# Residual transfers on GpSimd's queue, a buffer of their own for growing sums, a convolution that runs on into the last gate, and the output's first products by quarters

## The chip, the cores and the metric

The kernel runs on one core of a Trainium2 chip. TensorE (PE) multiplies, VectorE (DVE), ScalarE (ACT) and GpSimd (POOL) do the rest, and SyncE (SP) issues transfers. The metric is the device time of one execution in microseconds; of several runs the median is taken.

## The reference

A trunk of two layers (DEPTH = 2) over 512 tokens of 1024 channels, in float32. Cut to what matters here:

```python
for l in range(depth):
    h = _rmsnorm(x, g_mix[l])
    proj = h @ w_in[l]              # gates of 4 branches | conv | three attentions
    ys = jnp.stack([y_a, y_b, y_c, y_d], axis=2)   # conformer conv, three attentions
    branch = jnp.einsum('bsnc,ncd->bsnd', ys, w_branch[l])
    gates = jax.nn.sigmoid(gate_pre.reshape(bsz, seq, 4, 1024) + gate_b[l])
    mixed = jnp.sum(gates * branch, axis=2)
    x = x + mixed @ w_out[l]
    x = x + _conv_ffn(_rmsnorm(x, g_ffn[l]), w_up[l], ffn_conv_w[l], ffn_conv_b[l], w_down[l])
```

The FFN has 2816 channels in each half: up-projection, a depthwise convolution of width 3, silu(gate) times up, and the down-projection.

## The kernel before, in words

All activations lie transposed: 128 channels on the partitions, 512 tokens along the row, so the 1024 channels are eight tiles (d = 0 to 7). A float32 product is made of three products of rounded parts: `hi` (rounded) and `lo` (the rest), hi*hi + hi*lo + lo*hi. Each weight tile is loaded as `w_raw`, rounded on ScalarE into `w_hi` (L245 or L271), and VectorE makes `w_lo` (L247 or L272). `w_raw` is a ring of two tiles, `w_hi` and `w_lo` rings of three.

A layer runs: the norm and its projections; convolution and attentions as generators on a list `side`, of which `tick()` takes one step between matmuls; the gates of three branches; then `last_gate_and_out()`; then the norm of the FFN, its up-projections (44 blocks of 24 matmuls in `ffn`, two per step i) and the down-projection.

The last gate (keys `0a`, `0b`) and the output projection (`oa`, `ob`) are matrix products of 2 by 2 blocks in seven products instead of eight, in the order of the list LAST. A11, A12 and A22 use quarters of the weight as loaded. S3, S2 and S4 use sums of quarters, which grow in a tile `chain`: the first quarter comes from SyncE, each next one is added in place by an accumulating DMA on GpSimd (`grow`, L252). S1 uses the tile that A22 was loaded into, grown by another quarter; in the kernel before it is a `w_raw` tile. The activations' side needs sums as well: `input_forms` loads the residual (`xf`, L916) and makes `form` tiles for the last gate; `mixed_forms(j)`, called for each pair of mixed rows (j = 0 to 3, each 256 of the 1024 contracted channels), makes the `sums`, their rounded parts `mform` and the rounded rows `mpart` (L948, L949). A matmul of these products is at L972, 128 by 256.

`last_out` adds the residual (`xr`, loaded at L1070, added at L1057), stores the new one (`res`, L1063) and calls `norm_tile`, which makes `xh`, `xl` and the square `sq`. `broadcast_norm` then sums the squares over the partitions (L385), and takes three Newton steps for the inverse root on VectorE (`ms`, `rs_q`, `RB`, L389 and L329 to L334). The up-projections multiply unnormed data, and RB is applied when a block leaves PSUM (U, L1181). Four banks may wait for that. `weight_sums` reads four quarters of a down-projection weight (`quad`, L1237), forms their sums on VectorE (L1244 to L1247) and stores them (L1250) for later.

The order of the instructions on each engine is settled when the program is built: a scheduler places them by data and priority. Engines then run their rows in that order and wait for each other by semaphores. A DMA is a row on the queue of the engine that issues it.

## Time and profile before

| what | value |
|---|---|
| median of three runs | 1609.56 us (1606.7 to 1610.41) |
| profiled execution | 1608.74 us, its span 1607.0 us |
| mean granted TensorE clock | 0.986 |
| busy PE, DVE, ACT, POOL | 1564.0, 1322.6, 898.4, 199.5 us |
| `xf`, `xr` loads and `res` stores | 24 in each layer, 256 KB each, on SyncE |

The span is the time between the first and the last instruction that the profiler saw; the device time stands 1.74 us above it. "Busy" counts matmuls in a pipeline, so TensorE at 97% still has places in which it waits, and stretches at a lowered clock.

### The profile page before, as it was taken

Reading aid. Unit: us, or ns where it says so; the run is one execution under the profiler, and the core shown is the slowest. Engines: PE = TensorE matmul, PEld = TensorE weight load, DVE = VectorE, ACT = ScalarE, POOL = GpSimd, SP = SyncE. Lnnn points to the kernel's source line nnn. Section 1 sums busy time; section 2 is a strip of 40 time slices with the busy share of each in tenths; the row PEclk is TensorE's granted clock in tenths of the full one; section 3 lists DMA queues with packets and bytes.
Section 4 is the critical chain, followed back from the end, with each engine's and each line's share of the span. In section 5 each row is a group of like instructions: output and inputs, shape, how many; then the busy total and the mean of one; then the engine's idle time right before and its main releaser. Section 6 shows DMA issues by size and latency. Waiting matters only on the chain.

```text
span 1607.0 us, 21849 instructions
## 1 busy us (share of the span) xinstructions
PE 1564.0 (97%) x7698; PEld 1319.2 (82%) x7698; DVE 1322.6 (82%) x2236; ACT 898.4 (56%) x1516; POOL 199.5 (12%) x332
## 2 busy tenths in 40 slices
PE   9999999999879999999999999999988899999999
PEld 8888888888868888888888888887978788888887
DVE  6699988878779997796676899889696899977964
ACT  5778777455535543454458686764555454443642
POOL 0102002122101111100002020021221011111000
PEclk9999999999899999999999999999998899999999
DMA  7632322657655556576555322226566667655675
GB/s 231 183 106 77 89 74 80 209 131 171 173 182 177 194 187 200 197 235 210 182 184 179 108 79 84 72 87 209 138 165 183 197 199 224 212 197 199 222 222 169
DMA packets 110301, 265.94 MB, mean 165 GB/s; under 512 B 28272, under 2 KB 30192, under 8 KB 110192
## 3 DMA queue, kind: packets, MB, share of 16 engines
q1 hardware_dynamic: 91696, 200.57, 39.4%
q0 software_dynamic: 18208, 63.45, 14.4%
q8 instruction: 61, 1.00, 0.3%
q10 hardware_dynamic: 288, 0.52, 0.1%
q14 instruction: 48, 0.39, 0.1%
HBM read 223.60 MB, written 35.66 MB: 161 GB/s over the span
## 4 chain that ended last, share of the span: by engine, by line
PE 80%; DVE 11%; ACT 4%; DMA 2%; issue 2%; POOL 0%; SPq 0%; ACTq 0%; DVEq 0%
PE mm L302 15%; PE mm L300 15%; PE mm L301 15%; PE aux L972 6%; PE aux L1312 2%; PE aux L1313 2%; PE aux L1314 2%; PE mm L524 2%; PE mm L526 2%; PE mm L525 2%; DVE w_lo L247 2%; PE mm L1313 2%; PE mm L1312 2%; PE mm L1314 2%; PE aux L817 2%
## 5 line engine op out<-in xcount | busy, mean ns | idle before, releaser
L300 PE MATMUL mm<-xh,w_hi 128*128 128x512 f32 x1152 | 451.3, 392 | 15.4 <-ACT w_hi L245 8.2
L302 PE MATMUL mm<-xh,w_lo 128*128 128x512 f32 x1152 | 450.8, 391 | 0.6 <-DVE w_lo L247 0.5
L301 PE MATMUL mm<-xl,w_hi 128*128 128x512 f32 x1152 | 450.5, 391 | 0.0
L245 ACT ACTIVATE w_hi<-w_raw 128x1024 fp32r<-128x1024 f32 (+1 forms) x273 | 284.9, 1044 | 288.5 <-PE mm L301 104.4
L247 DVE TENSOR_TENSOR w_lo<-w_raw,w_hi 128x1024 fp32r<-128x1024 f32 (+1 forms) x273 | 329.7, 1209 | 88.1 <-ACT w_hi L245 84.9
L300 PEld LDWEIGHTS mm<-xh,w_hi 128*128 128x128 f32 x1152 | 217.4, 189 | 61.0 <-ACT w_hi L245 8.6
L302 PEld LDWEIGHTS mm<-xh,w_lo 128*128 128x128 f32 x1152 | 217.2, 189 | 47.3 <-DVE w_lo L247 1.8
L301 PEld LDWEIGHTS mm<-xl,w_hi 128*128 128x128 f32 x1152 | 217.4, 189 | 43.7 <-DVE xl L358 0.2
L895 POOL TENSOR_TENSOR mx<-mx,t 128x512 f32<-128x512 f32 x40 | 64.4, 1636 | 309.1 <-DVE t L894 196.9
L462 DVE SCALAR_TENSOR_TENSOR cv<-cv,prm 128x512 f32<-128x512 f32 x120 | 94.1, 784 | 0.6
L1181 DVE TENSOR_TENSOR U<-mm,RB 128x512 f32<-128x512 f32 x88 | 60.2, 688 | 38.4 <-PE mm L302 38.2
L1184 ACT ACTIVATE cy<-U,prm 128x512 f32<-128x512 f32 x88 | 70.7, 807 | 25.7 <-DVE U L1181 25.7
L524 PE MATMUL mm<-w_hi,xh 128*128 128x512 f32 x192 | 76.4, 398 | 0.4 <-DVE V L652 0.4
L525 PE MATMUL mm<-w_lo,xh 128*128 128x512 f32 x192 | 75.0, 390 | 0.0
L526 PE MATMUL mm<-w_hi,xl 128*128 128x512 f32 x192 | 74.8, 390 | 0.0
L781 ACT ACTIVATE e<-e,rl 128x256 f32<-128x256 f32 (+2 forms) x96 | 57.4, 598 | 21.8 <-DVE rl L780 21.4
L1186 DVE SCALAR_TENSOR_TENSOR cy<-U,prm,cy 128x512 f32<-128x512 f32 x88 | 65.6, 747 | 1.2
L1185 DVE SCALAR_TENSOR_TENSOR cy<-U,prm,cy 128x512 f32<-128x512 f32 x88 | 65.5, 746 | 0.0
L1190 ACT ACTIVATE fth<-cy 128x512 f32<-128x512 f32 x44 | 27.8, 632 | 66.6 <-DVE cy L1186 66.6
L1250 POOL DMA_DIRECT2D sums<-t x44 | 24.0, 546 | 311.4 <-DVE t L1244 292.0
L272 DVE TENSOR_TENSOR w_lo<-w_raw,w_hi 128x1024 fp32r<-128x1024 f32 x32 | 41.8, 1306 | 23.9 <-ACT w_hi L271 23.7
L972 PE MATMUL aux<-mform,w_hi 128*128 128x256 f32 x256 | 53.9, 309 | 5.8 <-DVE mform L949 2.1
(355 smaller groups left out, 3240.5 us busy)
## 6 DMA issues: line engine op xcount, KB each, us to landing
w_raw<-W SPq DMA_DIRECT2D x215, 512.0 KB, 3.7
quad<-W POOLq DMA_DIRECT2D x44, 512.0 KB, 5.2
w_raw<-W SPq DMA_DIRECT2D x66, 256.0 KB, 3.7
chain<-W POOLq DMA_DIRECT2D x24, 512.0 KB, 6.4
sums<-t POOLq DMA_DIRECT2D x44, 256.0 KB, 3.0
sums<-quad POOLq DMA_DIRECT2D x44, 256.0 KB, 3.8
w_raw<-sums SPq DMA_DIRECT2D x44, 256.0 KB, 3.9
w_raw<-sums SPq DMA_DIRECT2D x22, 512.0 KB, 4.6
```

Source lines behind the costliest of these rows:

```text
L245: w = nc.scalar.activation(hi[:, s], raw[:, s], AF.Copy)
L247: nc.vector.tensor_tensor(lo[:, s], raw[:, s], hi[:, s].bitcast(F32), ALU.subtract)
L300: mm(ps, lhsT=wh, rhs=xh, start=start, stop=False)
L301: mm(ps, lhsT=wh, rhs=xl, start=False, stop=False)
L302: self.last_mm = mm(ps, lhsT=wl, rhs=xh, start=False, stop=stop)
L462: self.after_mm(v.scalar_tensor_tensor(acc, u[:, t:t + S], w(t), acc, ALU.mult, ALU.add))
L524: mm(pss[b], lhsT=self.Xh[k][:, t], rhs=hi[:, s], start=k == 0, stop=False)
L525: mm(pss[b], lhsT=self.Xh[k][:, t], rhs=lo[:, s], start=False, stop=False)
L526: self.last_mm = mm(pss[b], lhsT=self.Xl[k][:, t], rhs=hi[:, s], start=False, stop=k == KT - 1)
L972: self.last_mm = self.nc.tensor.matmul(o, lhsT=a[:, s], rhs=x, start=start, stop=j == 3 and i == 2, skip_group_check=True)
L1184: nc.scalar.activation(y, u[:, 1:513], AF.Identity, scale=w(1), bias=self.par('ffn_conv_b', c))
L1186: v.scalar_tensor_tensor(y, u[:, 2:514], w(2), y, ALU.mult, ALU.add)
```

## The change

The residual loads (`xf`, `xr`) and the stores (`res`) are issued by GpSimd instead of SyncE. The tile of A22, which grows into that of S1, is `other`, one tile outside the ring. `form_sums` is a generator that stops after t3, and lays out t3 first; `mixed_forms` first rounds this quarter (256 columns) and the rows, then the other 768 columns, so that ScalarE and VectorE have one more instruction per j. The squares of the FFN norm take four tiles of another pool. The drain of the side generators before the last gate ends when the four forms stand, and what is left of `side` (the convolution) runs on during the gate and is drained after it. S1's sum is taken by halves in `0b` too. The first three output products run over j = 0 and 1, then 2, then 3, instead of 0 and 1, then 2 and 3. The first `weight_sums` comes at i = 1 instead of i = 0. TensorE has 7692 matmuls in both programs.

```diff
--- before.py
+++ after.py
@@ -264,7 +264,10 @@
         if n[0] == 'S':
             raw = self.chains[key] if n != 'S1' else self.others[key]
         else:
-            raw = self.wpool.tile([P, 1024], F32, name="w_raw", tag="w_raw", bufs=2)
+            if n == 'A22':
+                raw = self.op.tile([P, 1024], F32, name="other", tag="other", bufs=1)
+            else:
+                raw = self.wpool.tile([P, 1024], F32, name="w_raw", tag="w_raw", bufs=2)
             nc.sync.dma_start(raw, q[key, int(n[1]) - 1, int(n[2]) - 1])
         hi = self.wpool.tile([P, 1024], F32R, name="w_hi", tag="w_hi", bufs=3)
         lo = self.wpool.tile([P, 1024], F32R, name="w_lo", tag="w_lo", bufs=3)
@@ -362,7 +365,7 @@
             with self.tc.issue_after(self.first_hi.ins):
                 nc.scalar.activation(self.sqacc, xn, AF.Square)
         else:
-            sq = pool.tile([P, S], F32, name="sq", tag=self.sq_tag, bufs=2)
+            sq = pool.tile([P, S], F32, name="sq", tag=self.sq_tag, bufs=4 if self.sq_tag == "cv" else 2)
             nc.scalar.activation(sq, xn, AF.Square)
             nc.vector.tensor_tensor(self.sqacc, self.sqacc, sq, ALU.add)
 
@@ -898,12 +901,13 @@
 
     def form_sums(self, t, b11, b12, b21, b22):
 
-        t1, t2, t3, t4 = (t[:, n * 256:(n + 1) * 256] for n in range(4))
+        t3, t4, t2, t1 = (t[:, n * 256:(n + 1) * 256] for n in range(4))
         p = self.nc.vector.tensor_tensor
         p(t3, b12, b22, ALU.subtract)
-        p(t1, b11, b12, ALU.subtract)
+        yield
         p(t2, t3, b11, ALU.subtract)
         p(t4, b21, t2, ALU.add)
+        p(t1, b11, b12, ALU.subtract)
 
     def input_forms(self):
 
@@ -913,7 +917,7 @@
         for j in range(4):
             x = self.op.tile([P, 1024], F32, name="xf", tag=f"XR{j}", bufs=1)
             for e in range(2):
-                nc.sync.dma_start(x[:, e * S:(e + 1) * S], self.xres[2 * j + e])
+                nc.gpsimd.dma_start(x[:, e * S:(e + 1) * S], self.xres[2 * j + e])
             xs.append(x)
 
         def work():
@@ -923,7 +927,8 @@
                     nc.scalar.activation(x[:, s], x[:, s], AF.Copy, scale=self.par('g_mix', 2 * j + e))
                 yield
                 t = self.op.tile([P, 1024], F32, name="sums", tag=f"mt{j % 2}", bufs=1)
-                self.form_sums(t, *(x[:, n * 256:(n + 1) * 256] for n in range(4)))
+                for _ in self.form_sums(t, *(x[:, n * 256:(n + 1) * 256] for n in range(4))):
+                    pass
                 hi, lo = (self.op.tile([P, 1024], F32R, name="form", tag=f"xf{2 * j + n}", bufs=1) for n in range(2))
                 nc.scalar.activation(hi, t, AF.Copy)
                 nc.vector.tensor_tensor(lo, t, hi.bitcast(F32), ALU.subtract)
@@ -938,20 +943,29 @@
         v = nc.vector
         x, y = self.mixed[2 * j:2 * j + 2]
         t = self.op.tile([P, 1024], F32, name="sums", tag=f"XR{2 + j % 2}", bufs=1)
-        self.form_sums(t, x[:, :256], x[:, 256:], y[:, :256], y[:, 256:])
         tags = [f"mt{2 * j + n}" for n in range(2)] + [f"mb{2 * j + n}" for n in range(2)]
         if j >= 2:
             tags = [f"xf{4 * (j - 2) + n}" for n in range(4)]
         th, tl = (self.op.tile([P, 1024], F32R, name="mform", tag=t, bufs=1) for t in tags[:2])
         bh, bl = (self.op.tile([P, 768], F32R, name="mpart", tag=t, bufs=1) for t in tags[2:])
-        for h, l, s in ((th, tl, t), (bh[:, :256], bl[:, :256], x[:, :256]), (bh[:, 256:], bl[:, 256:], y)):
+
+        def parts(h, l, s):
             nc.scalar.activation(h, s, AF.Copy, scale=0.5)
             v.scalar_tensor_tensor(l, s, 0.5, h.bitcast(F32), ALU.mult, ALU.subtract)
+
+        sums = self.form_sums(t, x[:, :256], x[:, 256:], y[:, :256], y[:, 256:])
+        next(sums)
+        parts(th[:, :256], tl[:, :256], t[:, :256])
+        parts(bh[:, :256], bl[:, :256], x[:, :256])
+        parts(bh[:, 256:], bl[:, 256:], y)
+        for _ in sums:
+            pass
+        parts(th[:, 256:], tl[:, 256:], t[:, 256:])
         self.mforms.append(((th, tl), (bh, bl)))
 
     def seven_x(self, key, n, j):
 
-        form = {'S1': 0, 'S2': 1, 'S3': 2, 'A22': 3}.get(n)
+        form = {'S1': 3, 'S2': 2, 'S3': 0, 'A22': 1}.get(n)
         if form is not None:
             return [t[:, form * 256:(form + 1) * 256] for t in (self.forms[j] if key[0] == '0' else self.mforms[j][0])]
         if key[0] == 'o':
@@ -984,7 +998,7 @@
         w = self.unit()
         for e in range(2):
             self.seven_part(key, n, w, range(4), e)
-            if key == 'ob' and n == 'S1':
+            if key[1] == 'b' and n == 'S1':
                 self.seven_sum(key, n, e)
             if e == 0:
                 self.tick()
@@ -992,7 +1006,7 @@
         if n in ('S3', 'A11'):
             self.seven_copy(key, n)
             return
-        if not (key == 'ob' and n == 'S1'):
+        if not (key[1] == 'b' and n == 'S1'):
             self.seven_sum(key, n)
         done(key, n)
 
@@ -1060,14 +1074,14 @@
         for e in range(2):
             d = 4 * g + 2 * (1 - r) + e
             xn = xr[:, e * S:(e + 1) * S]
-            nc.sync.dma_start(self.xnew[d], xn)
-            self.norm_tile(d, xn, self.op)
+            nc.gpsimd.dma_start(self.xnew[d], xn)
+            self.norm_tile(d, xn, self.gp)
 
     def load_residual(self, q):
 
         x = self.op.tile([P, 1024], F32, name="xr", tag=f"XR{q}", bufs=1)
         for e in range(2):
-            self.nc.sync.dma_start(x[:, e * S:(e + 1) * S], self.xres[2 * q + e])
+            self.nc.gpsimd.dma_start(x[:, e * S:(e + 1) * S], self.xres[2 * q + e])
         self.xrs.append(x)
 
     def last_gate_and_out(self):
@@ -1086,18 +1100,21 @@
             self.seven(key, n, self.last_gate)
         for d in (6, 7):
             self.branch(ORDER[3], d, bu, self.ths[d])
+        while self.side:
+            self.tick()
         for q in range(4):
             self.load_residual(q)
         self.xnew = self.new_res()
+        self.sq_tag = "cv"
         self.start_norm('g_ffn')
         ws = []
+        for js in ((0, 1), (2,), (3,)):
+            for i, (key, n) in enumerate(steps[at:at + 3]):
+                if js[0] == 0:
+                    ws.append(self.unit())
+                for e in range(2):
+                    self.seven_part(key, n, ws[i], js, e)
         for key, n in steps[at:at + 3]:
-            ws.append(self.unit())
-            for e in range(2):
-                self.seven_part(key, n, ws[-1], (0, 1), e)
-        for (key, n), w in zip(steps[at:at + 3], ws):
-            for e in range(2):
-                self.seven_part(key, n, w, (2, 3), e)
             if n != 'A12':
                 self.seven_copy(key, n)
             else:
@@ -1170,7 +1187,7 @@
                 pss.append(self.mm())
                 self.block(pss[s])
                 self.tick()
-            if i % 2 == 0:
+            if i % 2 == 0 and i or i == 1:
 
                 with self.tc.issue_after(self.last_mm.ins):
                     self.weight_sums(l, i // 2)
@@ -1529,7 +1546,7 @@
                 self.after.append(lambda: self.grow(self.chains['0a'], self.quarters[l]['0a', 0, 0]))
                 for _ in third:
                     pass
-                while self.side:
+                while len(self.forms) < 4:
                     self.tick()
                 self.last_gate_and_out()
                 self.broadcast_norm()
```

SyncE's and GpSimd's queues around the stores of layer 0. SyncE before, from the second-last weights of `w_out` to the first weights of the up-projection (L241; L268 loads the blocks of the seven products, L257 starts a chain):

```order
L257 DMA chain<-W 128x1024
L268 DMA w_raw<-W 128x1024 x2
L1070 DMA xr<-xT 128x512 x4
L268 DMA w_raw<-W 128x1024 x2
L1063 DMA res_4400<-xr 128x512
L1063 DMA res_4401<-xr 128x512
L1063 DMA res_4402<-xr 128x512
L1063 DMA res_4403<-xr 128x512
L241 DMA w_raw<-W 128x1024 x3
L1063 DMA res_4404<-xr 128x512
```

Here the first four stores stand ahead of the first three weights of the up-projection. GpSimd before, up to the memsets of U behind which the first two quads come:

```order
L252 DMA chain<-W 128x1024 x2
L252 DMA w_raw<-W 128x1024
L252 DMA chain<-W 128x1024 x2
L252 DMA w_raw<-W 128x1024
L252 DMA chain<-W 128x1024
L1162 MEMSET U_4922 128x1
```

GpSimd has only growing tiles here; `w_raw` is the one that grows from A22 into S1. SyncE after, the same stretch (L271 is the old L268, for `other` and `w_raw`):

```order
L241 DMA w_raw<-W 128x1024
L271 DMA w_raw<-W 128x1024
L271 DMA other<-W 128x1024
L271 DMA w_raw<-W 128x1024
L257 DMA chain<-W 128x1024
L271 DMA w_raw<-W 128x1024 x2
L271 DMA other<-W 128x1024
L241 DMA w_raw<-W 128x1024 x44
```

On SyncE nothing is left but weights. GpSimd after (L1084 is the old L1070, L1077 the old L1063), from the last loads of `xr` to the fourth of the eight stores:

```order
L252 DMA chain<-W 128x1024 x2
L1084 DMA xr<-xT 128x512 x2
L1077 DMA res_4409<-xr 128x512
L1077 DMA res_4410<-xr 128x512
L252 DMA other<-W 128x1024
L252 DMA chain<-W 128x1024
L1077 DMA res_4411<-xr 128x512
L1077 DMA res_4412<-xr 128x512
```

The stores and the xr loads have left SyncE, and stand on GpSimd between the growing tiles and after them. The first quads (L1254, x2) follow the stores and the memsets of U.

VectorE in layer 0, from the sum of squares to the first U. Before (L329 to L334 are the Newton steps, L247 a weight's `w_lo`, L1244 to L1247 the sums of the quad):

```order
L334 SCALAR_TENSOR_TENSOR RB<-rs_q,RB 128x512
L1246 TENSOR_TENSOR t_5026<-quad 128x512
L332 SCALAR_TENSOR_TENSOR rs_q<-RB 128x512
L247 TENSOR_TENSOR w_lo<-w_raw,w_hi 128x1024
L333 TENSOR_TENSOR rs_q<-rs_q,ms 128x512
L1247 TENSOR_TENSOR quad<-quad,t_5026 128x512
L334 SCALAR_TENSOR_TENSOR RB<-rs_q,RB 128x512
L332 SCALAR_TENSOR_TENSOR rs_q<-RB 128x512
L333 TENSOR_TENSOR rs_q<-rs_q,ms 128x512
L334 SCALAR_TENSOR_TENSOR RB<-rs_q,RB 128x512
L247 TENSOR_TENSOR w_lo<-w_raw,w_hi 128x1024
L1181 TENSOR_TENSOR U_4922<-mm,RB 128x512
```

Two weight splits and four sums of the quad (two of them in these rows) stand between the steps. After (L332 to L337 are the Newton steps, L1198 the old L1181, L1261 the old L1244):

```order
L336 TENSOR_TENSOR rs_q<-rs_q,ms 128x512
L337 SCALAR_TENSOR_TENSOR RB<-rs_q,RB 128x512
L335 SCALAR_TENSOR_TENSOR rs_q<-RB 128x512
L336 TENSOR_TENSOR rs_q<-rs_q,ms 128x512
L337 SCALAR_TENSOR_TENSOR RB<-rs_q,RB 128x512
L247 TENSOR_TENSOR w_lo<-w_raw,w_hi 128x1024
L335 SCALAR_TENSOR_TENSOR rs_q<-RB 128x512
L336 TENSOR_TENSOR rs_q<-rs_q,ms 128x512
L337 SCALAR_TENSOR_TENSOR RB<-rs_q,RB 128x512
L1198 TENSOR_TENSOR U_4931<-mm,RB 128x512
L1198 TENSOR_TENSOR U_4934<-mm,RB 128x512
L1261 TENSOR_TENSOR t_5110<-quad 128x512
```

The sums of the quad have gone behind the first two U, and one weight split fewer stands between the steps.

TensorE at the first output products of layer 0. Before, with the numbers of the tiles (`mform_4309` and `_4310`, `mpart_4311` and `_4312` belong to j = 2, `mpart_4380` to j = 3):

```order
L972 MATMUL aux_4416<-mform_4309,w_hi_4319 128x256
L972 MATMUL aux_4435<-mpart_4311,w_hi_4412 128x256
L972 MATMUL aux_4435<-mpart_4312,w_hi_4412 128x256
L972 MATMUL aux_4435<-mpart_4311,w_lo_4413 128x256
L972 MATMUL mm_4455<-mpart_4311,w_hi_4431 128x256
L972 MATMUL mm_4455<-mpart_4312,w_hi_4431 128x256
L972 MATMUL mm_4455<-mpart_4311,w_lo_4432 128x256
L972 MATMUL aux_4416<-mform_4310,w_hi_4319 128x256
L972 MATMUL aux_4416<-mform_4309,w_lo_4320 128x256
L972 MATMUL aux_4435<-mpart_4380,w_hi_4412 128x256
L972 MATMUL mm_4455<-mpart_4380,w_hi_4431 128x256
```

The last two rows belong to j = 3. After (`mpart_4312` and `_4313` belong to j = 2, `mpart_4383` and `_4384` to j = 3):

```order
L986 MATMUL aux_4444<-mpart_4312,w_lo_4422 128x256
L986 MATMUL mm_4464<-mpart_4312,w_hi_4440 128x256
L986 MATMUL mm_4464<-mpart_4313,w_hi_4440 128x256
L986 MATMUL mm_4464<-mpart_4312,w_lo_4441 128x256
L986 MATMUL mm_4464<-mpart_4312,w_hi_4440 128x256
L986 MATMUL mm_4464<-mpart_4313,w_hi_4440 128x256
L986 MATMUL mm_4464<-mpart_4312,w_lo_4441 128x256
L986 MATMUL aux_4444<-mpart_4383,w_hi_4421 128x256
L986 MATMUL aux_4444<-mpart_4384,w_hi_4421 128x256
L986 MATMUL aux_4444<-mpart_4383,w_lo_4422 128x256
L986 MATMUL aux_4444<-mpart_4383,w_hi_4421 128x256
```

Before, the first matmuls of j = 3 stand between those of j = 2, after nine of them; in the new order j = 2 is whole, 18 matmuls, before j = 3 begins.

## The prediction

> **What bounds the kernel now.** I read the head of the page first, then TensorE's waits, then the windows around them, and last the instructions inside four of those windows.
>
> ```profile
> span 1607.0 us, 21849 instructions
> PE 1564.0 (97%) x7698; PEld 1319.2 (82%) x7698; DVE 1322.6 (82%) x2236; ACT 898.4 (56%) x1516; POOL 199.5 (12%) x332
> ```
>
> TensorE is busy 97% of the span. The change adds and removes no matmul, so all that it can win is TensorE's idle time, and the time that matmuls lose to the half clock granted after an idle stretch. Four rows of the waits (us in total, times, longest):
>
> ```profile
> PE mm L300 <- ACT w_hi L245: 8.2, 2, 5.1
> PE aux L500 <- DVE cv L491: 7.5, 2, 3.9
> PE mm L300 <- DVE U L1181: 7.2, 2, 4.1
> PE aux L972 <- DVE sv L1021: 2.6, 2, 1.3
> ```
>
> Each comes twice, once per layer. The fifth place in a layer is where L972 waits several times for the forms of the output's first products. Windows around the five (the third value is PE busy; PEclk is the granted clock, 1.00 being full):
>
> ```profile
> core 0: us, PE busy (x) PEld busy (x) DVE busy (x) ACT busy (x) POOL busy (x), PEclk, DMA share, GB/s
> 324.00:332.00 8.00, 4.06 (x16) 3.10 (x15) 7.34 (x15) 0.98 (x1) 2.46 (x2) 0.79 0.39 129
> 381.00:390.00 9.00, 7.24 (x45) 5.83 (x45) 9.00 (x13) 4.68 (x6) 0.00 (x0) 1.00 0.51 145
> 399.00:417.00 18.00, 13.09 (x64) 11.15 (x63) 13.27 (x20) 8.00 (x11) 2.60 (x3) 0.72 0.55 136
> 442.00:451.00 9.00, 3.78 (x14) 2.82 (x14) 2.78 (x5) 1.06 (x1) 0.00 (x0) 0.81 0.39 153
> 476.00:480.00 4.00, 0.86 (x4) 0.66 (x4) 3.97 (x6) 1.83 (x3) 0.25 (x1) 1.00 0.84 288
> 1121.00:1130.00 9.00, 5.47 (x22) 4.05 (x21) 7.34 (x13) 4.64 (x7) 1.75 (x2) 0.81 0.35 117
> 1179.00:1188.00 9.00, 7.21 (x45) 5.81 (x44) 9.00 (x13) 5.14 (x6) 0.02 (x1) 1.00 0.50 152
> 1198.00:1216.00 18.00, 13.19 (x60) 11.35 (x59) 12.79 (x19) 7.77 (x11) 2.60 (x3) 0.62 0.56 135
> 1241.00:1250.00 9.00, 5.37 (x23) 4.52 (x23) 3.68 (x7) 2.11 (x2) 0.00 (x0) 0.81 0.38 144
> 1273.00:1284.00 11.00, 6.94 (x19) 5.21 (x18) 10.90 (x17) 6.54 (x8) 0.54 (x1) 0.69 0.77 228
> ```
>
> Idle is the width less PE busy: 3.94, 1.76, 4.91, 5.22, 3.14 in layer 0 and 3.53, 1.79, 4.81, 3.63, 4.06 in layer 1, together 36.8 us. The half clock costs at most width times (1 - PEclk): 1.7, 0, 5.0, 1.7, 0 and 1.7, 0, 6.8, 1.7, 3.4, together 22 us. So the ceiling of any gain is 59 us.
>
> **The change part by part.**
>
> *First up-projection weight (windows 442 and 1241).* TensorE waits there for a weight that is still in flight:
>
> ```profile
> 421.70 1.23 DVE L272 TENSOR_TENSOR w_lo<-w_raw,w_hi 128x1024 fp32r<-128x1024 f32 x1 [1.66 <-ACT w_hi L271]
> 427.70 6.62 SPq L1063 DMA_DIRECT2D res<-xr  x4
> 433.45 1.13 DVE w_lo L272
> 433.58 1.16 POOL L1237 DMA_DIRECT2D quad<-W  x2
> 434.62 11.34 DMA w_raw<-W
> 447.17 0.73 PE L300 MATMUL mm<-xh,w_hi 128*128 128x512 f32 x1 [5.12 <-ACT w_hi L245]
> ```
>
> The load leaves at 434.62, when ob's A12 split (433.45 + 1.13) frees its ring slot; A22 holds the other slot until S1 is split. Two 512 KB quads left 1 us earlier, and the load needs 11.34 us. In the new kernel A22 is out of the ring, so the slot of the split at 421.70 is free at 422.93, 11.7 us earlier; the four residual stores no longer stand ahead of it on SyncE; and the quads come behind the eight stores on GpSimd. Even from the old slot, without the quads, the load would make it by 442. The whole loss goes: 5.22 + 1.7 and 3.63 + 1.7 = 12.3 us. I take 11.5, for some clock lost otherwise; at the least 5, if the load still meets other transfers.
>
> *First gate of the FFN norm (windows 476 and 1273).* TensorE has filled its PSUM banks and waits for U, which needs the Newton chain on VectorE:
>
> ```profile
> 472.19 1.22 DVE L247 TENSOR_TENSOR w_lo<-w_raw,w_hi 128x1024 fp32r<-128x1024 f32 x1
> 473.93 0.68 DVE L1247 TENSOR_TENSOR quad<-quad,t 128x512 f32<-128x512 f32 x1
> 477.31 1.22 DVE L247 TENSOR_TENSOR w_lo<-w_raw,w_hi 128x1024 fp32r<-128x1024 f32 x1
> 478.44 1.88 DVE L1181 TENSOR_TENSOR U<-mm,RB 128x512 f32<-128x512 f32 x3
> 479.28 0.47 PE L300 MATMUL mm<-xh,w_hi 128*128 128x512 f32 x1 [3.14 <-DVE U L1181]
> ```
>
> With `weight_sums(0)` one block later, the four quad sums (L1244 to L1247, spaced 0.60) leave this chain, and one of its weight splits (1.13) too: 2.4 + 1.1 = 3.5 us, against a wait of 3.14. Layer 1 loses the same and one transpose less inside (0.6): 4.2 against 4.06, and its 3.4 of half clock with it. I take 3.0 + 6.0 = 9 us, between 5.5 (no clock regained, a split remaining) and 10.6. TensorE's order between the last product of `ob` and the waiting matmul is the same in both kernels, so an earlier start shifts the chain and the wait alike. The delayed first sums are used only in the down-projection, forty blocks later; their delay costs nothing.
>
> *First output products (windows 399 and 1198).* VectorE sets the pace:
>
> ```profile
> 403.87 0.58 PE L972 MATMUL aux<-mpart,w_hi 128*128 128x256 f32 x1 [1.74 <-ACT mpart L948]
> 405.23 0.68 DVE L949 SCALAR_TENSOR_TENSOR mpart<-mx,mpart 128x512 fp32r<-128x512 f32 x1
> 409.22 1.22 DVE L949 SCALAR_TENSOR_TENSOR mform<-sums,mform 128x1024 fp32r<-128x1024 f32 x1
> 412.74 1.28 PE L972 MATMUL aux<-mform,w_hi 128*128 128x256 f32 x4 [1.03 <-ACT w_hi L271]
> ```
>
> The last form is whole only at 410.44. S3 needs a quarter of it; in the new order that quarter and the parts stand ahead of the other 768 columns, and j=3's inputs would be ready at about 406, where the last parts end now (405.23 + 0.68). The products by quarters give 18 more matmuls of 0.12 us (2.2 us) that can run before j=3. Against this stand 8 more instructions each on ScalarE and VectorE (0.1 us or so apiece beyond the columns that they share), and a new tight spot: A22's split can start only when A11's last matmul has freed its slot, twelve matmuls (1.4 us) ahead of use, while a w_hi and a w_lo take 1.06 + 1.22. VectorE's sum of work stays. I take 3 and 4 us, 7 in all, out of 4.9 + 5.0 and 4.8 + 6.8; the ends are 0 (VectorE no earlier) and 16 (three quarters of both).
>
> *Convolution run into the last gate (windows 324 and 1121, and 381 and 1179).* The transposes L500 wait for L491, behind a VectorE chain that began with a late input:
>
> ```profile
> 298.47 8.70 DMA xf<-xT
> 327.63 1.45 DVE L491 TENSOR_SCALAR cv<-aux,mv,rln 128x256 f32<-128x256 f32 x3
> ```
>
> The order of the new kernel puts the same VectorE work ahead of L491 and the first L500 four or five matmuls (some 1 us) earlier on TensorE. So ending the drain early brings no cover. An earlier xf could give 2 us back: its loads now leave from GpSimd instead of behind weights on SyncE. I take 0 for each layer, from a gain of 0.5 to a loss of 1.5. The S1 sum of 0b by halves (L1021, 1.3 us of wait per layer) is still waited for as a pair by S4's first matmul: 0, to a loss of 0.7 per layer.
>
> *Residual transfers on GpSimd.* 48 DMAs leave SyncE for a queue on which the growing sums stand too:
>
> ```profile
> 401.60 9.69 SPq L1070 DMA_DIRECT2D xr<-xT  x4
> 409.60 0.86 POOL L252 DMA_DIRECT2D w_raw<-W  x1 [16.40 <-DVE w_lo L272]
> 417.73 1.06 ACT L271 ACTIVATE w_hi<-w_raw 128x1024 fp32r<-128x1024 f32 x1 [4.07 <-PE aux L972]
> 438.38 1.06 ACT L271 ACTIVATE w_hi<-chain 128x1024 fp32r<-128x1024 f32 x1 [1.56 <-DMA chain<-W]
> L1250 POOL DMA_DIRECT2D sums<-t x44 | 24.0, 546 | 311.4 <-DVE t L1244 292.0 <-DVE t L1246 18.6 <-DVE fl L1294 0.8
> w_raw<-W POOLq DMA_DIRECT2D x8, 512.0 KB, 5.7
> ```
>
> An issue takes 0.546 us, so 48 of them are 26 us on an engine that is 12% busy: off the path by themselves. What matters is the order: two xr loads stand ahead of oa's `other` grow, and today those loads wait for their tiles up to about 411. The grow would leave at 411.5 instead of 409.60 and land 5.7 later, at 417.2; ScalarE takes it at 417.73. Ahead of ob's last grows stand two stores, 1.1 us; the S4 weight arrives at 438.38 today, is split 2.3 us later, and TensorE needs it after 442. Both hide with 0.5 to 1.3 us to spare, so I charge 1.5 us in all for them and the tight spot above, 0 to 6.
>
> The Trainium skill (SBUF — State Buffer, the box "The DVE blocks DMA trap (SWDGE)") speaks against this part: a DMA issued from GpSimd has its descriptors written by GpSimd's cores, and a two-port VectorE instruction can lock them out. The trace does not show it: L1250's issues take 0.546 us on average with VectorE busy 82% of the span. If each moved issue waited out one 1.22 us split, the 48 would cost 85 us of GpSimd instead of 26 by this estimate; the sum above goes by 26.
>
> **Sum.** -11.5 - 9 - 7 + 0 + 1.5 = -26 us. The profiled execution took 1608.74 us, 1.74 around its span of 1607.0; the median of the runs, 1609.56, is 0.8 above it. 1608.74 - 26 + 0.8 is 1583.5 us. With all terms at their good ends it is 1569, at their bad ends 1609.
>
> **The rivals.** *VectorE keeps the pace of the output products*: the quarter form comes no earlier since VectorE comes to them without a gap, the slow clock stays, and the convolution loses 1.5 us per layer. That is -11.5 - 9 + 0 + 3 = -17.5 and 1592 us. For it: DVE is 9.00 of 9.00 busy in the 381 window. Against: of 18 us in the 399 window it is busy only 13.27.
>
> *Nearly the ceiling*: once TensorE no longer stops in 399 to 417, the clock is never lowered there, and 17 of those 21.5 us come back: 1608.74 - 11.5 - 10 - 17 + 0.8 = 1571 us. For it: every window of PEclk below 0.82 lies behind an idle stretch. Against: 476 to 480 lost 3.14 us at clock 1.00, so idle time and lowered clock aren't tied one to one, and the new split stands on the path.
>
> *The transfers share what they shared*: if the load of 11.34 us was slow because of all transfers together and not because of its place, moving 256 KB stores to another queue changes nothing. Then -7 to -10 remain, and 1601 us. For it: at 476 to 480, with quads in flight, the DMA share is 0.84 at 288 GB/s. Against: eight transfers of the same 512 KB from GpSimd land in 5.7 us, half of 11.34, and the free slot lets this one start before the quads. The Trainium skill (DMA: Bandwidth & Descriptors, "Issuing engines are not separate DMA queues") says that DMAs of all issuing engines run on the same 16 DMA engines and interleave, so that another issuer saves only issue time. By it the gain must come from the slot and the order, as I have counted it.
>
> *GpSimd's queue in order blocks the weights* (slower): an xr load or a store waits for VectorE, and the grow behind it with it. There are three such places per layer (oa's `other`, ob's `other`, ob's last chain), hidden by 0.5 to 1.3 us today. Each us beyond is TensorE's. At 6 us late in all six, less the 1 hidden, 30 us are lost: 1583.5 + 30 = 1613 us; below 5.5 us late it doesn't turn the sign. For it: oa's grow clears by only 0.5. Against: the first store leaves at 427.70 today, 11 us before ScalarE takes ob's last chain at 438.38.
>
> **How the numbers follow.** Forecast 1583.5 (its own range 1577 to 1589): 0.52. VectorE's pace, 1592: 0.22. Nearly the ceiling, 1571: 0.12. Transfers unchanged, 1601: 0.08. Blocked queue, 1613: 0.06. A change of 0.2% (3.2 us) is about what a measurement of this kernel can tell. Faster holds the first four but for a part of the last: 0.90; same 0.04; slower 0.06. The range 1571 to 1600 leaves out the slower case, half of the transfers' case and the better half of the ceiling's.
>
> **What the changed profile would show.** Right: no wait of L300 for w_hi L245 near 436, and its load leaving ahead of the first quad; the wait of L300 for U (now L1198) under 1 us; S3, A11 and A12 of oa running through j=2 with PEclk above 0.8 in the window that is 0.72 and 0.62 now; L500's wait unchanged at 3 to 5 us. Wrong: a wait of L986 (the old L972) for w_hi behind a DMA `other<-W` or `chain<-W`, a wait of L500 over 5 us, or the same idle time moved a few matmuls on, which would show as equal windows at other lines.

## The result, and the profile after

The changed kernel takes 1589.15 us (median of four runs, 1586.98 to 1591.63) against 1608.13 us before (1604.49 to 1610.41): ratio 0.9885, 95% interval 0.9859 to 0.991. The forecast was 1583.5 us in a range of 1571 to 1600: the direction and the range held, the gain is 19 us where 26 were forecast. The profiled execution has a span of 1585.2 us, 21.8 less than before; it is the fastest of the four (1586.98 us), so the profiles differ by more than the medians, whose difference is 19.0 us. Both profiles hold 7698 matmuls (not 7692, as the description of the change has it).

The waits of TensorE, with the new line numbers (L503 is the old L500, L986 the old L972, L1198 the old L1181, L303 and L305 the old L300 and L302):

```profile
PE aux L503 <- DVE cv L494: 10.9, 2, 6.0
PE aux L986 <- ACT sv L1017: 4.8, 4, 1.3
PE aux L986 <- DVE sv L1035: 3.2, 2, 1.6
PE mm L305 <- DVE w_lo L247: 2.9, 2, 1.7
PE aux L986 <- DVE mpart L954: 2.9, 2, 1.4
PE aux L986 <- ACT mpart L953: 1.9, 2, 1.0
PE mm L303 <- DVE U L1198: 1.0, 2, 0.7
```

The wait for the first up-projection weight (8.2) has no row any more, that for U has fallen from 7.2 to 1.0, and the wait of the conv transposes has risen from 7.5 to 10.9. The windows around the same five places in each layer:

```profile
322.00:334.00 12.00, 5.99 (x23) 4.62 (x22) 9.79 (x22) 6.54 (x9) 1.80 (x2) 0.72 0.27 87
382.00:390.00 8.00, 5.07 (x34) 3.90 (x32) 8.00 (x13) 4.75 (x7) 0.76 (x1) 1.00 0.50 179
404.00:414.00 10.00, 6.51 (x38) 5.90 (x37) 9.08 (x16) 6.02 (x9) 2.02 (x3) 0.83 0.27 66
440.00:444.00 4.00, 2.33 (x16) 1.80 (x15) 3.78 (x6) 0.12 (x1) 0.00 (x0) 1.00 0.09 7
468.00:470.00 2.00, 1.73 (x9) 1.14 (x7) 1.93 (x4) 0.52 (x1) 0.00 (x0) 1.00 0.77 262
1110.00:1122.00 12.00, 7.12 (x25) 5.29 (x24) 8.52 (x18) 5.79 (x8) 1.27 (x1) 0.72 0.25 87
1172.00:1180.00 8.00, 5.06 (x32) 3.89 (x31) 8.00 (x14) 3.91 (x6) 0.00 (x0) 1.00 0.45 144
1194.00:1202.00 8.00, 4.31 (x20) 3.90 (x20) 6.98 (x13) 4.85 (x8) 2.02 (x3) 0.79 0.19 67
1230.00:1232.00 2.00, 0.77 (x5) 0.66 (x5) 2.00 (x4) 0.00 (x0) 0.00 (x0) 1.00 0.00 0
1258.00:1260.00 2.00, 1.26 (x6) 1.07 (x7) 2.00 (x3) 2.00 (x3) 0.00 (x0) 1.00 0.49 96
```

Read as in the prediction (idle is width less PE busy, the half clock at most width times 1 - PEclk), the two layers together give, in us:

| place | idle, half clock before | idle, half clock after | change | forecast |
|---|---|---|---|---|
| conv transposes | 7.5, 3.4 | 10.9, 6.7 | +6.7 | 0 |
| 0b's second half | 3.6, 0 | 5.9, 0 | +2.3 | 0 |
| output's first products | 9.7, 11.9 | 7.2, 3.4 | -11.0 | -7 |
| first up weight | 8.9, 3.4 | 2.9, 0 | -9.4 | -11.5 |
| first U | 7.2, 3.4 | 1.0, 0 | -9.6 | -9 |
| GpSimd's queue, spread over these | | | | +1.5 |
| sum | | | -21.0 | -26 |

The sum is within 1 us of the span's 21.8, so in sum little is left for the rest of the program. The largest miss against the forecast is the first row.

What holds the transposes up is seen two steps back. GpSimd's queue in layer 0, and VectorE behind it:

```profile
284.63 0.54 POOL L920 DMA_DIRECT2D xf<-xT  x1 [1.38 <-ACT ytmp L830]
297.27 0.91 POOL L252 DMA_DIRECT2D chain<-W  x1 [12.10 <-DMA other<-W]
300.37 0.60 POOL L920 DMA_DIRECT2D xf<-xT  x1
301.52 1.46 POOL L920 DMA_DIRECT2D xf<-xT  x2
310.25 0.72 ACT L927 ACTIVATE xf<-xf,prm 128x512 f32<-128x512 f32 x1 [2.17 <-DMA xf<-xT]
313.44 1.22 DVE L934 TENSOR_TENSOR form<-sums,form 128x1024 fp32r<-128x1024 f32 x1 [3.41 <-ACT form L933]
328.80 0.47 PE L503 MATMUL aux<-cst,cv 128*128 128x128 f32 x1 [6.01 <-DVE cv L494]
```

Five of the eight xf loads leave by 285. Then the first growing sum is at the head of the queue and waits 12.10 us for a weight to land, and the last three loads stand behind it. The first of the three leaves 16 us after the fifth, ScalarE and VectorE wait for them, and VectorE comes late to L494. The same place before:

```profile
298.47 3.42 SPq L916 DMA_DIRECT2D xf<-xT  x5
307.95 0.66 DVE L903 TENSOR_TENSOR sums<-xf 128x256 f32<-128x256 f32 x1 [0.99 <-ACT xf L923]
309.27 0.43 DVE L903 TENSOR_TENSOR sums<-xf 128x256 f32<-128x256 f32 x1 [0.67 <-ACT xf L923]
311.83 1.22 DVE L929 TENSOR_TENSOR form<-sums,form 128x1024 fp32r<-128x1024 f32 x1 [0.33 <-ACT form L928]
328.23 0.69 PE L500 MATMUL aux<-cst,cv 128*128 128x128 f32 x2 [3.94 <-DVE cv L491]
```

The last five xf loads left SyncE in one row from 298.5 on, and VectorE waited 2.0 us in three pieces, where it waits 3.41 now. This is only a part of the longer wait. The first L494 now starts at 328.20 and the first L491 started at 327.63, 0.6 us earlier, while TensorE stands at the transposes at 322.8 (328.80 less 6.01) instead of 324.3. The traces have 1542 matmuls ahead of them in layer 0 where there were 1547, and 5394 where there were 5398 in layer 1. At 0.23 us from one such matmul to the next, the nine that now come behind the waits are 2 of the 3.4 us by which the waits grew.

### The profile page after: what moved, and what is told of

It reads as the page before. It is cut to its first block, busy times and chain, and to the rows that moved or that the text cites. A ratio compares the mean times of both kernels' runs of the same rounds, so it can differ in the third digit from the quotient of the medians.

```text
span 1585.2 us, 21881 instructions
## 1 busy us (share of the span) xinstructions
PE 1551.2 (98%) x7698; PEld 1309.8 (83%) x7698; DVE 1320.5 (83%) x2246; ACT 898.1 (57%) x1524; POOL 223.4 (14%) x380
## 4 chain that ended last, share of the span: by engine, by line
PE 80%; DVE 10%; ACT 4%; DMA 3%; issue 2%; POOL 1%; SPq 0%; ACTq 0%; POOLq 0%; DVEq 0%
PE mm L303 15%; PE mm L305 15%; PE mm L304 15%; PE aux L986 6%; PE aux L1331 3%; PE aux L1330 3%; PE aux L1329 3%; PE mm L527 2%; PE mm L529 2%; PE mm L528 2%; PE mm L1331 2%; PE mm L1329 2%; PE mm L1330 2%; DVE w_lo L247 2%; PE aux L820 2%
## 5 line engine op out<-in xcount | busy, mean ns | idle before, releaser
L305 PE MATMUL mm<-xh,w_lo 128*128 128x512 f32 x1152 | 450.6, 391 | 2.9 <-DVE w_lo L247 2.9
L303 PE MATMUL mm<-xh,w_hi 128*128 128x512 f32 x1152 | 450.2, 391 | 1.0 <-DVE U L1198 1.0
L247 DVE TENSOR_TENSOR w_lo<-w_raw,w_hi 128x1024 fp32r<-128x1024 f32 (+1 forms) x273 | 329.1, 1207 | 79.9 <-ACT w_hi L245 78.8
L305 PEld LDWEIGHTS mm<-xh,w_lo 128*128 128x128 f32 x1152 | 217.0, 188 | 49.5 <-DVE w_lo L247 3.8
L303 PEld LDWEIGHTS mm<-xh,w_hi 128*128 128x128 f32 x1152 | 216.7, 188 | 45.8 <-issue 2.2
L1198 DVE TENSOR_TENSOR U<-mm,RB 128x512 f32<-128x512 f32 x88 | 60.0, 685 | 23.4 <-PE mm L305 23.3
L784 ACT ACTIVATE e<-e,rl 128x256 f32<-128x256 f32 (+2 forms) x96 | 57.4, 598 | 21.8 <-DVE rl L783 21.4
L777 ACT ACTIVATE e<-e,nm 128x256 f32<-128x256 f32 (+2 forms) x96 | 57.6, 600 | 2.7
L805 DVE TENSOR_TENSOR pt<-aux,pt 128x256 fp32r<-128x256 f32 (+2 forms) x96 | 50.8, 530 | 2.4 <-ACT pt L804 1.3
```

The source lines that it names most:

```text
L247: nc.vector.tensor_tensor(lo[:, s], raw[:, s], hi[:, s].bitcast(F32), ALU.subtract)
L303: mm(ps, lhsT=wh, rhs=xh, start=start, stop=False)
L305: self.last_mm = mm(ps, lhsT=wl, rhs=xh, start=False, stop=stop)
```

## The experiments

Two theories for the lost 6.7 us: A, the xf loads are held up in a queue; B, the run-on convolution brings TensorE to L503 sooner. The first two runs undo one part of the change each.

**xf loads back on SyncE.** In `input_forms`:

```diff
-                nc.gpsimd.dma_start(x[:, e * S:(e + 1) * S], self.xres[2 * j + e])
+                nc.sync.dma_start(x[:, e * S:(e + 1) * S], self.xres[2 * j + e])
```

> The changed kernel with the eight xf loads of each layer back on SyncE; xr loads and res stores stay on GpSimd. In the changed kernel the transposes L503 wait 6.0 and 4.9 us for L494 (3.9 and 3.5 before), and with the half clock the two places lose 9.4 and 8.3 us instead of 5.6 and 5.2. Theory A (GpSimd's queue in order): the last xf loads leave late, behind an addition that waits for VectorE, VectorE idles 3.4 us for the forms, and that is the loss. Then the wait comes back to 4 us or less in each layer, and the time falls by 4 to 7 us, to 1582 to 1585 us. Theory B (TensorE reaches L503 earlier, since the convolution runs on into the gate): the wait stays at 5 us or more and the time within 2 us. Half and half: about 5 us of wait, 2 to 3 us of time.

1588.64 us, ratio to before 0.9876 (0.9857 to 0.9895): no different from the changed kernel. The transposes wait 9.9 us in all, 6.9 of it in layer 0 and 3.0 in layer 1. Theory A in this form holds at most in layer 1, where the wait falls from 4.9 to 3.0; in layer 0 SyncE held the loads up just as well. Its queue in layer 0 shows how:

```profile
292.81 0.42 SPq L271 DMA_DIRECT2D other<-W  x1
293.28 0.43 SPq L920 DMA_DIRECT2D xf<-X  x1
297.99 0.33 SPq L241 DMA_DIRECT2D w_raw<-W  x1
298.36 4.14 SPq L920 DMA_DIRECT2D xf<-xT  x7
307.83 0.42 DVE L906 TENSOR_TENSOR sums<-xf 128x256 f32<-128x256 f32 x1 [4.46 <-ACT xf L927]
```

A22 now has its tile as soon as the pool opens, so its 512 KB load is placed ahead of the xf loads; one xf load leaves before the weight that waits, where three did before, and VectorE waits 4.46 us.

**The full drain restored.** Before `last_gate_and_out()`:

```diff
-                while len(self.forms) < 4:
+                while self.side:
```

> The changed kernel with the full drain of the side generators before the last gate, as before the change; all else as changed. Theory B (the run-on convolution costs): the wait of L503 for L494 falls by 1 us or more in each layer, and the time by 2 to 6 us. Theory A (the xf loads on GpSimd cost): the wait stays within 0.5 us of 6.0 and 4.9 and the time within 2 us of 1589. A third case: the run-on was worth something elsewhere in the gate, and the time rises by 2 us or more.

1589.08 us, ratio 0.9885 (0.9868 to 0.9903), the wait 12.2 us in all (5.7 and 6.5; the second is further from 4.9 than theory A had allowed). So the run-on convolution neither costs nor brings anything that these runs can tell, and theory B is refuted. TensorE comes to the transposes of layer 0 as early as in the changed kernel, after 1542 matmuls, so it is not the run-on that brought it there sooner. The next thing to try is the place of the loads in the order.

**xf loads first, on GpSimd.** The changed kernel, with

```diff
-                nc.gpsimd.dma_start(x[:, e * S:(e + 1) * S], self.xres[2 * j + e])
+                with self.first():
+                    nc.gpsimd.dma_start(x[:, e * S:(e + 1) * S], self.xres[2 * j + e])
```

> The changed kernel with the eight xf loads given priority, so that on GpSimd all eight stand ahead of the first two chain grows (in the changed kernel three of them stand behind these, and the first grow waits 12.1 us for loads of A22 and the chain). Theory A, refined (the last xf loads are held up by the grows ahead of them in GpSimd's queue; with xf on SyncE they were held up by the early other load instead, 4.5 us of VectorE idle in layer 0): VectorE's idle time before the forms (3.4 and 2.6 us) goes to under 1 us, the wait of L503 falls by 2 us or more in each layer, and the time by 4 to 8 us, to 1581 to 1585 us. Theory D (the wait of L503 is VectorE's amount of work and TensorE's earlier arrival): VectorE's idle time goes, but the wait falls by less than 1 us in each layer and the time by less than 2 us.

1581.94 us, ratio 0.9834 (0.9813 to 0.9856). GpSimd's queue now reads

```profile
284.76 3.17 POOL L921 DMA_DIRECT2D xf<-xT  x6 [2.44 <-ACT ytmp L830]
297.33 0.91 POOL L252 DMA_DIRECT2D chain<-W  x1 [9.41 <-DMA chain<-W]
```

and the transposes wait half as long, 5.2 us in both layers (the first row of its waits):

```profile
PE aux L503 <- DVE cv L494: 5.2, 2, 3.3
```

VectorE's 3.41 us before the form are gone. The wait fell by 2.7 and 3.0 us, and 7 us of time came back, as refined theory A expected; theory D is refuted. TensorE is at the transposes of layer 0 at 322.9, after 1542 matmuls, as in the changed kernel, so that nearly all of the 2.7 us there is VectorE's: its first L494 starts at 325.6 instead of 328.2.

**xf loads first, on SyncE.** The same with `nc.sync.dma_start` under `with self.first():`.

> The same as the kernel with the xf loads first on GpSimd, but they are first on SyncE's queue, ahead of the chain and other loads. If the place in the order decides and not the queue: the waits of L503 within 1 us in each layer of the 3.3 and 1.8 us with the loads first on GpSimd, and 1580 to 1584 us. If GpSimd's queue is itself better or worse for these loads: a difference of 2 us or more in the wait of a layer. On SyncE the loads stand behind fifteen weights that wait for their ring slots, so they may come some us later; if that matters, VectorE idles again before the forms.

1579.57 us, ratio 0.9824 (0.9809 to 0.9839), the lowest of all kernels run. The wait is 5.0 us in both layers together (3.1 and 1.9), within 0.2 of that with GpSimd. Its queue in layer 0:

```profile
266.76 25.47 SPq L241 DMA_DIRECT2D w_raw<-W  x5
292.32 0.38 SPq L921 DMA_DIRECT2D xf<-X  x1
292.76 3.29 SPq L921 DMA_DIRECT2D xf<-xT  x7
298.31 0.43 SPq L257 DMA_DIRECT2D chain<-W  x1
298.78 0.43 SPq L271 DMA_DIRECT2D other<-W  x1
```

Here too the loads stand behind weights that wait, and leave 11 us later than the first ones on GpSimd; but all eight have left by 296.1, ahead of `chain` and `other`, while the last two of the changed kernel leave from 301.5 on. Which engine issues them makes no difference that these two runs show; when the last of the eight has left does.

**The changed kernel once more**, on the same chip as the run above.

> The changed kernel itself, on the same chip as the two above, for a comparison with them, and to see how steady the half clock is at the output's first products (1.7 us of loss in each layer in its first profile; 0 to 5.1 in the variants with the same instructions there). Expected: 1587 to 1590 us, the same waits within 0.3 us, and half-clock losses that differ from the first profile by some us where the waits don't.

1589.02 us, ratio 0.9885 (0.9868 to 0.9902). The same program, and yet the transposes wait 5.9 and 7.5 us in this profile, where they waited 6.0 and 4.9 in the first. The row of VectorE in layer 1 gives the reason, first in the changed kernel's first profile, then in this one:

```profile
1093.60 1.23 DVE L934 TENSOR_TENSOR form<-sums,form 128x1024 fp32r<-128x1024 f32 x1 [2.61 <-ACT form L933]
```

```profile
1099.29 1.23 DVE L934 TENSOR_TENSOR form<-sums,form 128x1024 fp32r<-128x1024 f32 x1 [6.86 <-ACT form L933]
```

An xf load of this layer took up to 9.2 us to land in the first and 11.0 in the second, and ScalarE waited 4.0 and 7.2 us for such loads. VectorE idled 4 us more, and the transposes waited 2.6 us more. The loss follows the landing of xf. It also means that one profile tells this wait to some 2 us only; the verdicts on the runs with full drain and with xf on SyncE rest on the times beside it.

Four parts were put into the kernel before alone, to size the terms.

**The tile of its own.** A22 in `other`, and the squares in the other pool (`sq` with four tiles, `norm_tile(d, xn, self.gp)`), since the tile has no room otherwise (alone it needs a pool of 100 KB per partition where 96 are left, so that there is no time for it alone):

```diff
+            if n == 'A22':
+                raw = self.op.tile([P, 1024], F32, name="other", tag="other", bufs=1)
+            else:
```

> The kernel before with A22 in a tile of its own outside the ring, and the squares of the FFN norm in the other pool, without which the tile has no room; all transfers stay on SyncE. Slot theory for the first up-projection weight: the ring slot frees the load some 12 us earlier, the first load stands ahead of the stores on SyncE, and the waits of 5.1 and 3.1 us go below 1.5 us each: 7 to 10 us off 1608. Queue theory: half the wait or more remains, 0 to 5 us off. At the conv transposes: SyncE now loads other ahead of the xf tiles; theory A says that the wait of L500 grows by 0.5 to 2 us in a layer, theory B that it stays at 3.9 and 3.5.

1598.8 us, ratio 0.9946 (0.9926 to 0.9967). Its waits:

```profile
PE aux L503 <- DVE cv L494: 10.0, 2, 6.8
PE mm L305 <- DVE w_lo L247: 2.8, 2, 1.7
```

The wait for the weight itself is gone without moving a store; 2.8 us for its `w_lo` are what is left, as in the changed kernel (2.9). The slot theory holds, though one of these waits is 1.7 us, over the 1.5 expected. And the transposes of layer 0 already wait 6.8 instead of 3.9, with all transfers on SyncE: in this layer the tile alone brings the wait of the changed kernel. Layer 1 went from 3.5 to 3.2.

**The transfers on GpSimd**, all 48, and nothing else (three `nc.sync` to `nc.gpsimd`, as in the change).

> The kernel before with the 48 residual transfers on GpSimd's queue, and nothing else. If the transfers share what they shared: within 3 us of 1608 and the wait for the first up-projection weight (5.1 and 3.1 us) within 1 us of before. If SyncE's order was part of that wait: the stores no longer stand ahead, the wait falls by half, 3 to 6 us off. If GpSimd's order in itself blocks: the wait of L500 at the conv transposes rises by 1 us or more in each layer, 2 to 6 us more, and the wait for the first weight hardly moves.

1604.74 us, ratio 0.9978 (0.9964 to 0.9992).

```profile
PE aux L500 <- DVE cv L491: 10.9, 2, 6.3
PE mm L300 <- DVE U L1181: 8.0, 2, 4.3
PE mm L300 <- ACT w_hi L245: 3.4, 2, 1.7
```

Parts of two expectations came true at once: the weight's wait falls by more than half (8.2 to 3.4), and the transposes' rises (7.5 to 10.9), to 4.6 us in layer 0 and 6.3 in layer 1. So the tile delays xf in layer 0, and the move to GpSimd mostly in layer 1. This part alone is worth 0.2%; in the whole change its gain is probably already had by the tile, since both act on the same wait.

**Quad sums one step later.** `if i % 2 == 0 and i or i == 1:` in `ffn`.

> The kernel before with one edit: the first weight_sums comes at i = 1 instead of i = 0. The place is the first U of the FFN (waits of 3.1 and 4.1 us, and 3.4 us of half clock in layer 1). If the four quad sums inside the Newton chain are the cause: waits of 1 us or less each, 6 to 9.5 us off 1608. If the wait comes from the whole chain being late with the first weight: waits of 2.5 us or more remain, less than 4 us off.

1600.76 us, ratio 0.9952 (0.9935 to 0.997). The row of the wait:

```profile
PE mm L300 <- DVE U L1181: 1.8, 2, 1.6
```

Of 7.2 us 1.8 are left, 1.6 of them in layer 1, where 1 or less was expected. The quad sums in the Newton chain were the cause of the rest.

**Products by quarters** alone (`form_sums`, `mixed_forms`, `seven_x` and the loop over `js` of the change).

> The kernel before with the output's first products by quarters: the order of form_sums, the split of mixed_forms, and the products over j = 0 and 1, then 2, then 3. The window around them loses 10.0 us (idle 4.9, half clock 5.1) in layer 0 and 11.7 in layer 1; in the changed kernel 5.2 and 5.4. If this edit alone did it: 5 us off in each layer, 9 to 12 us off 1608. If the run-on convolution, the halves of S1 or the transfers share in it: 3 us off or less in each layer. As to 0b's waits (the window of 1.8 us in each layer, 2.8 and 2.9 in the changed kernel): if the split forms lengthen them, they rise here by 0.5 to 1 us.

1601.69 us, ratio 0.9961 (0.9944 to 0.9978). The window's idle time goes from 4.9 and 4.8 to 3.9 and 4.0 us, and its half clock from 5.0 and 6.8 to 5.1 and 1.7. One of the waits is longer than any before:

```profile
404.87 1.07 PE L983 MATMUL aux<-mpart,w_hi 128*128 128x256 f32 x2 [2.45 <-ACT mpart L950]
```

TensorE waits for the first inputs of j = 3 all the same: VectorE and ScalarE are not there. So here the edit saves 0.8 to 1.0 us of idle time a layer, and 5 us of lowered clock in this profile. But over the whole program this profile lost 22.2 us to the lowered clock, as much as the one of before: what the clock gained here it lost at other places. Where the rest of the 7 us comes from is not shown. 0b's windows stay at 1.6 and 1.5.

**S1's sum whole in 0b**, in the kernel with the xf loads first on GpSimd:

```diff
-            if key[1] == 'b' and n == 'S1':
+            if key == 'ob' and n == 'S1':
```

(and the same condition further down).

> The kernel of the run before it with the xf loads first on GpSimd's queue, and S1's sum of 0b whole again (the change's halves kept for ob alone). The window of the last gate's second half loses 2.8 to 3.0 us per layer in every variant with the change, 1.7 to 1.8 before it and 1.5 to 1.6 with the quarters alone: a new wait of 1.2 us for a copy of ScalarE, and 1.6 instead of 1.3 us for S1's sum. If the halves cause it: 1 us or so less per layer, 1580 us against 1582. If another edit does (the order of mixed_forms together with the convolution): the window keeps 2.7 us or more and the time is within 1.5 us of 1582.

1580.9 us, ratio 0.9834 (0.9818 to 0.985). 0b's windows go from 2.9 and 2.8 to 1.6 us each, so the halves cause that loss: S1's sum is waited for 0.4 us instead of 1.6. The new wait for a copy of ScalarE stays (1.2 us); it is there with the products by quarters alone as well (1.4 and 1.5). But the next window, of the output's first products, idles 4.1 and 4.0 us instead of 3.4 each. 0.6 us a layer remain, and no difference that the times can tell from the 1581.94 with halves.

## Why the prediction was right or wrong

*First up weight, -11.5: right in its cause, 2 too much.* -9.4. The load leaves at 422.36, near the 422.93 that was worked out. What was not charged is the order on ScalarE and VectorE:

```profile
422.36 25.43 SPq L241 DMA_DIRECT2D w_raw<-W  x4
437.50 1.06 ACT L274 ACTIVATE w_hi<-chain 128x1024 fp32r<-128x1024 f32 x1 [1.56 <-DMA chain<-W]
439.06 1.06 ACT L245 ACTIVATE w_hi<-w_raw 128x1024 fp32r<-128x1024 f32 x1
441.66 1.22 DVE L247 TENSOR_TENSOR w_lo<-w_raw,w_hi 128x1024 fp32r<-128x1024 f32 x1
442.94 0.50 PE L305 MATMUL mm<-xh,w_lo 128*128 128x512 f32 x1 [1.67 <-DVE w_lo L247]
```

The load left long before, but the weight's rounding stands behind the last chain's, which waits for its grow, and its `w_lo` comes another 1.5 us after the rounding, behind the chain's and three sums on VectorE. I had looked at that 1.56 us and called it hidden, since nobody needed the chain's product that early; the ones behind it in the queues needed the engines. No run changes this order, so this reading rests on the rows.

*First U, -9: right.* -9.6 in the profile, and with this part alone 6.8 by the medians (1607.6 to 1600.76), or 4.8 to 10.5 by the interval of the ratio.

*Output's first products, -7: the amount came out, not its reason.* I had split it as inputs of j = 3 ready earlier. The 18 more matmuls that were to run ahead of j = 3 are nine, by the two orders shown ahead of the prediction: nine of j = 2 ran ahead of it before and 18 do now. The idle time fell by only 2.5 us in both layers (9.7 to 7.2), and it is still the parts of j = 3 that are late (L953 and L954, 1.0 and 1.4 us in each layer); the rest is a wait for a copy of ScalarE (L1017, 1.1 and 1.3 us). The other 8.5 are half clock. In the six profiles that have the change's instructions here, in this kernel and its variants, idle time is 3.4 to 3.8 us a layer, while the half clock of both layers together is 3.4, 5.1, 3.4, 1.7, 8.5 and 6.8 us. In the four profiles that have the old instructions here (the kernel before, and with the tile, the transfers or the late quad sums alone) it is 11.9, 10.2, 13.7 and 10.2 us. So there is a gain, but its size is not steady, and that the sum came out at the -7 forecast and more is in part luck.

*Convolution and xf, 0: the step that failed.* +6.7. The text had the right pieces: the transposes wait behind a chain that began with a late xf, and the grows and the residual transfers share a queue. It then let the xf loads "leave from GpSimd instead of behind weights on SyncE" and credited them with up to 2 us, without reading what stands ahead of them there: two grows, the first of which waits for loads. The rival of a blocked queue was named with three other places (both `other` grows and the last chain), where it hid; at the fourth, in front of the xf loads, it struck. That `other` may be loaded ahead of xf, as soon as the pool opens, was not seen at all. And the text had seen that its order put the transposes "four or five matmuls (some 1 us) earlier on TensorE", yet charged nothing for it: this is 1.1 and 0.9 us of wait. Of the 6.7 us 3.4 are wait and 3.3 lowered clock. The prediction's own sign of being wrong, a wait here over 5 us, came in layer 0 with 6.0.

*0b's halves, 0 to 1.4: +2.3*, outside its bound; the last run shows that the halves cost 1.2 to 1.3 us a layer and give half of that back further on.

*GpSimd's issues, 26 us off the path: right.* The 16 stores took 0.552 us each, as L1250's 0.546 had it:

```profile
L1077 POOL DMA_DIRECT2D res<-xr x16 | 8.7, 552 | 51.5 <-DVE xr L1071 51.4
```

The lock of which the Trainium skill warns (SBUF — State Buffer, "The DVE blocks DMA trap (SWDGE)") was not seen with this kernel's VectorE instructions: issues kept their time with VectorE busy 83% of the span. What cost time was the order of the queue.

*The rivals.* "VectorE keeps the pace", at 1592 us, came nearer in time than the forecast and is half true: idle time at the output's products moved by only 2.5 us, but the slow clock did not stay, and the convolution lost 6.7 us and not 3. "Transfers share what they shared" is refuted by the tile's run: the weight's wait goes without a transfer moving. The Trainium skill's rule (DMA: Bandwidth & Descriptors, "Issuing engines are not separate DMA queues") agrees with the two runs with xf first: 5.2 and 5.0 us of wait by either engine.

Alone, the four parts gain 0.54, 0.22, 0.48 and 0.39%, together 1.63% or 26 us: what was forecast, though each of the four is known only to about 0.2%. The whole change gains 1.15%. The gain of the transfers overlaps with the tile's, and each of these two delays xf, the tile in layer 0 and the transfers mostly in layer 1. With the xf loads first on SyncE the gain over the kernel before is 1.76% (1.61 to 1.91).

## What to carry to other kernels

When a transfer moves to another engine's queue, read what stands ahead of it there and what those rows wait for: a queue in order passes on the wait of its head, and an engine that is 14% busy can hold a load up for 16 us. A buffer that is given its own place can be filled earlier, and that early load goes ahead of something else, as in layer 0 here; give the load that the critical chain begins with a priority. And an instruction whose product is not needed yet is not free to wait, if the next one on its engine is.

## What was not expected of the hardware

The lowered clock does not follow idle time closely. It came in pieces: where the clock was lowered it was at half, and in every trace for 3.4 us or a whole multiple of it (but for the end of the program), so that each loss above is 1.7 us or a multiple of it, as near as the two digits of PEclk give it. The same instructions around the output's first products lost 1.7 to 8.5 us to it in both layers together, at idle times that agreed within 0.4 us a layer; the waits of 1.2 and 1.6 us in 0b's windows left the clock at 1.00 in the first profile of the changed kernel, and lowered it for 1.7 us of loss in layer 0 of the second. Over all the program (the span times 1 less the mean granted clock) the loss was 22 us before and 10 after in the first profiles, so about half of the 21.8 us of span is clock; in the second profile of the changed kernel it was 14. The kernel before and the four with one part of the change lost 18.8 to 25.9 us, the seven profiles with the whole change or nearly all of it 8.5 to 13.7. That TensorE stops less often and for shorter times may be the reason; no run separates the two.
